# Attention as woven lists of steps with a stated matmul order, a merged softmax and values in two passes

## The chip, the cores and the metric

The kernel runs on one core of a Trainium2 chip. The metric is device time in microseconds (us), the median of several runs. Engines: PE is TensorE (matmuls and transposes), DVE is VectorE, ACT is ScalarE, POOL is GpSimd, and SP is SyncE, which issues most DMAs. Each engine takes its instructions strictly in the order of its own list.

## The reference, cut to what matters

Two layers over 512 latent tokens of width 1024, in f32. Layer 0 is attention: each latent query sees a neighbourhood of the grid (with a learned bias) and 256 context keys in one softmax. Layer 1 is a spatial gating unit; a squared-ReLU MLP follows each. Shifts, scales and gates come from a conditioning vector.

```python
q, k, v = jnp.split(h @ w_qkv, 3, axis=-1)
q = rms_norm(heads(q), q_g)
k = rms_norm(heads(k), k_g)
...
s_lat = jnp.einsum('bjqhd,bkjmhd->bhjqkm', q_r, k_r,
                   preferred_element_type=jnp.float32) * scale + bias[None].astype(jnp.float32)
s_ctx = jnp.einsum('bjqhd,blhd->bhjql', q_r, kc,
                   preferred_element_type=jnp.float32) * scale
s = jnp.concatenate([s_lat.reshape(s_lat.shape[:4] + (n_lat_keys,)), s_ctx], axis=-1)
p = jax.nn.softmax(s, axis=-1).astype(v.dtype)
...
o = (jnp.einsum('bhjqkm,bkjmhd->bjqhd', p_lat, v_r)
     + jnp.einsum('bhjql,blhd->bjqhd', p_ctx, vc))
...
y = y.transpose(1, 0, 2, 3).reshape(bsz, n_tok, D_MODEL) @ w_o
x = x + g1 * y
x = x + g2 * squared_relu_mlp(modulate(rms_norm(x, norm2_g[i]), sh2, sc2), mlp_w1[i], mlp_w2[i])
```

## The kernel before, in words

**Numbers.** Every f32 operand is split in two parts that the fast matmul takes, `hi` (a rounded copy by ACT) and `lo` (the rest, a subtract by DVE). `products` (L183) multiplies such pairs with three matmuls: high by high, high by low, low by high. Weights come in units of 1536 columns by DMA (`raw`), are split into `whi` (ACT, L80) and `wlo` (DVE, L81) four pieces at a time, and lie in three buffers.

**Stages.** A start (to about 71 us) normalises the input and makes the projections of pair 0. Attention follows, then the output projection (`residual("o", ...)`), the MLP of layer 0, the gating unit, the MLP of layer 1.

**Attention** works on 8 pairs of heads. For a pair, `a_tile` multiplies 6 token tiles (4 latent with 384 columns of q, k and v, 2 context with 256 of k and v) by 8 pieces of weights in a bank of tag "mm", and empties the bank: squares, a raw copy, the values as `vh` and `vl`, sums of squares. `a_final` normalises, then `split` transposes three groups through the two banks of tag "t" (L417): context keys, latent keys, queries; ACT and DVE split each, and 16 small DMAs on SP's queue place the parts for the score matmuls. `scores(n)` does one head: for each of 4 query blocks two matmuls give 512 scores (256 latent, 256 context) in a bank of tag "s"; DVE takes the maximum of the context half (L461) and, with the bias added, that of the latent half (L462), ACT two exponentials (L465, L467), DVE adds the sums and inverts (L469, L470), and POOL scales the block in `pbuf`. `values(n)` does one head: for 6 key tiles, `turn` transposes the weights of 2 to 4 query blocks (L496), ACT and DVE split them into `ph` and `pl` (L499, L500), and `products` multiplies them with the values. The stationary operand is the head's 64 columns beside 64 columns of zeros, and both heads of a pair add up in one bank of tag "o".

**Conditioning products.** Beside this, `ada_block` loads 512 KB of conditioning weights into a single buffer `adaraw` by SP's queue and reduces them on DVE (L338); 24 of the 80 are done in attention, each tied behind a tile's sum of squares.

**Order.** The program calls `scores`, `values`, `a_tile` and `a_final` by pairs, and a scheduler decides at build time, by its own account of times, how their instructions stand in each engine's list. The output projection opens its first four blocks together (`first=4`), three in "mm" banks; the scheduler puts their matmuls among the last heads.

## Time and profile before

| | us |
|---|---|
| median of 3 runs | 1554.05 |
| lowest and highest | 1551.54, 1558.43 |
| the profiled execution | 1556.16 |
| its span, first to last instruction | 1554.4 |

The profile is one execution. Its page shows each engine's busy time over the span; windows show the same for a stretch; groups collect the instructions of a line and operation, with busy time, mean and the idle time before them; the timeline has single instructions. A matmul's length in the timeline includes its passage through the array, and the next one starts well before its end, so the distance of two starts tells what one costs. PEld are weight loads. The granted clock of PE is 1.00 of 2.4 GHz all through attention.

### The profile page before, as it was taken

To read this page: it belongs to the slowest core of one execution; us is meant where nothing else is said; L and a number is where in the kernel's file an instruction comes from. 1 tells how busy PE (TensorE), PEld (TensorE's weight loads), DVE (VectorE), ACT (ScalarE), POOL (GpSimd) and SP (SyncE) were. 2 spreads that over 40 slices of the span, in tenths; PEclk is the share of its full clock that TensorE was granted. 3 is DMA by queue.
4 is the path that set the end of the run, shared out by engine and by line. 5 is a ranking of instruction groups with operands and counts; after the bars stand their busy time and mean duration, and the time that the engine had idled before them with its cause. 6 is when DMAs were issued, how large, how long until landed. Compare 5 with 4: busy or idle time off the path is not lost.

```text
span 1554.4 us, 21486 instructions
## 1 busy us (share of the span) xinstructions
PE 1508.7 (97%) x7960; PEld 1290.6 (83%) x7960; DVE 925.4 (60%) x1953; ACT 663.6 (43%) x1569; POOL 135.8 (9%) x162
## 2 busy tenths in 40 slices
PE   3999999999999999999999999999999999999999
PEld 2898888887888888878978887888889988888888
DVE  5778777776776555765565568644456743334431
ACT  3566666675554312442343356323234542234320
POOL 0222222211200000000100013100001000000000
PEclk9999999999999999999999999999999999999999
DMA  9465555544246555555234235323221422223230
GB/s 321 145 177 169 164 167 162 164 115 161 74 143 202 187 199 191 197 196 191 85 125 135 98 100 166 123 90 111 93 95 42 143 102 93 90 102 102 99 112 27
DMA packets 69224, 212.08 MB, mean 136 GB/s; under 512 B 8320, under 2 KB 27392, under 8 KB 68736
## 3 DMA queue, kind: packets, MB, share of 16 engines
q1 hardware_dynamic: 57600, 200.57, 39.5%
q10 hardware_dynamic: 11520, 10.15, 2.1%
q8 instruction: 62, 1.02, 0.3%
q14 instruction: 42, 0.34, 0.1%
HBM read 193.91 MB, written 2.10 MB: 126 GB/s over the span
## 4 chain that ended last, share of the span: by engine, by line
PE 55%; DMA 12%; DVE 5%; issue 2%; ACT 0%; ACTq 0%; DVEq 0%
PE ps_mm L183 27%; PE ps_t L183 18%; DMA adaraw<-ada 11%; PE ps_o L183 9%; DVE adaraw L338 2%; PE ps_s L713 1%; DVE wlo L81 1%; DVE nt L172 0%; DMA raw<-wall 0%; DVE xall L569 0%; PE ps_s L156 0%; DVE acc L151 0%; DVE hl L174 0%; DVE relu L620 0%; DVE mod L338 0%
## 5 line engine op out<-in xcount | busy, mean ns | idle before, releaser
L80 ACT CAST whi<-raw 128x384 fp32r<-128x384 f32 x620 | 278.3, 510 | 358.0 <-PE ps_mm L183 142.1
L81 DVE TENSOR_TENSOR wlo<-raw,whi 128x384 fp32r<-128x384 f32 x620 | 329.5, 579 | 146.0 <-ACT whi L80 145.7
L338 DVE CUSTOM_DVE_ANT_0 adaraw<-adaraw,cb 128x1024 f32<-128x1024 f32 x80 | 99.2, 1240 | 105.0 <-DMA adaraw<-ada 104.9
L183 PE MATMUL ps_mm<-hh,wlo 128*128 128x512 f32 (+1 forms) x416 | 154.0, 370 | 0.6 <-DVE wlo L81 0.6
L183 PE MATMUL ps_mm<-hh,whi 128*128 128x512 f32 (+1 forms) x416 | 154.2, 371 | 0.0
L183 PE MATMUL ps_mm<-hl,whi 128*128 128x512 f32 (+1 forms) x416 | 153.8, 370 | 0.0
L183 PE MATMUL ps_mm<-whi,hh 128*128 128x384 f32 (+1 forms) x344 | 122.4, 358 | 4.0 <-ACT hh L289 4.0
L183 PE MATMUL ps_mm<-mh,whi 128*128 128x512 f32 (+1 forms) x336 | 121.4, 361 | 2.2 <-ACT mh L623 2.2
L183 PE MATMUL ps_mm<-wlo,hh 128*128 128x384 f32 (+1 forms) x344 | 122.1, 355 | 0.1
L183 PE MATMUL ps_mm<-ml,whi 128*128 128x512 f32 (+1 forms) x336 | 121.4, 361 | 0.2 <-DVE ml L624 0.2
L183 PE MATMUL ps_mm<-whi,hl 128*128 128x384 f32 (+1 forms) x344 | 121.5, 356 | 0.0
L183 PE MATMUL ps_mm<-mh,wlo 128*128 128x512 f32 (+1 forms) x336 | 121.1, 360 | 0.0
L183 PE MATMUL ps_t<-hh,whi 128*128 128x512 f32 (+1 forms) x280 | 104.4, 373 | 0.0
L183 PE MATMUL ps_t<-hl,whi 128*128 128x512 f32 (+1 forms) x280 | 104.2, 372 | 0.0
L183 PE MATMUL ps_t<-hh,wlo 128*128 128x512 f32 (+1 forms) x280 | 103.9, 371 | 0.0
L183 PEld LDWEIGHTS ps_mm<-hh,wlo 128*128 128x128 f32 x416 | 78.4, 189 | 13.8 <-DVE wlo L81 0.8
L183 PEld LDWEIGHTS ps_mm<-hl,whi 128*128 128x128 f32 x416 | 78.5, 189 | 12.6
L183 PEld LDWEIGHTS ps_mm<-hh,whi 128*128 128x128 f32 x416 | 78.5, 189 | 12.6
L623 ACT CAST mh<-relu 128x512 fp32r<-128x512 f32 x64 | 39.7, 621 | 99.8 <-DVE relu L620 99.8
L183 PEld LDWEIGHTS ps_mm<-mh,whi 128*128 128x128 f32 x336 | 63.7, 190 | 12.2 <-ACT mh L623 2.7
L183 PEld LDWEIGHTS ps_mm<-whi,hh 128*128 128x128 f32 x344 | 65.2, 190 | 9.0 <-ACT hh L289 4.4
L183 PEld LDWEIGHTS ps_mm<-ml,whi 128*128 128x128 f32 x336 | 63.9, 190 | 10.2 <-DVE ml L624 0.5
(217 smaller groups left out, 3303.6 us busy)
## 6 DMA issues: line engine op xcount, KB each, us to landing
raw<-wall SPq DMA_DIRECT2D x155, 768.0 KB, 4.5
adaraw<-ada SPq DMA_DIRECT2D x80, 512.0 KB, 3.9
aw<-ada SPq DMA_DIRECT2D x32, 256.0 KB, 7.1
bt<-bias_t SPq DMA_DIRECT2D x16, 512.0 KB, 3.5
q<-th SPq DMA_DIRECT2D x32, 128.0 KB, 2.4
q<-tl SPq DMA_DIRECT2D x32, 128.0 KB, 2.4
bc<-lngb ACTq DMA_DIRECT2D x12, 256.0 KB, 3.4
x0l<-x0T SPq DMA_DIRECT2D x2, 1024.0 KB, 9.3
```

The costliest lines, as they stand in the source:

```text
L80: nc.scalar.copy(out=hi[:, cs], in_=raw[:, cs])
L81: nc.vector.tensor_tensor(out=lo[:, cs], in0=raw[:, cs], in1=hi[:, cs], op=ALU.subtract)
L183: pe.matmul(o, lhsT=a, rhs=b, start=start and i == 0, stop=stop and i == n - 1, skip_group_check=shared)
L338: vec.tensor_tensor_reduce(out=a, in0=a, in1=cb, scale=1.0, scalar=0.0, op0=ALU.mult, op1=ALU.add, accum_out=mod[:, idx:idx + 1])
L623: act.copy(out=a, in_=r)
L713: pe.matmul(s[:, n * P:(n + 1) * P], lhsT=v[:, n, g * P:(g + 1) * P], rhs=ws, start=True, stop=True)
```

## The change

- **Values.** `vv` holds, for a token tile, high and low values side by side: for head 0 as (high, low), for head 1 as (low, high). One head's 128 columns are the stationary operand of two matmuls, with `ph` and with `pl`; the sum of the high part stands in one half of the bank's partitions and that of the low part in the other. `finish` copies the low half to `side` (ACT) and adds it to the high half (DVE), once for each head, and so the bank "o" belongs to one head at a time.
- **Softmax.** One DVE pass over all 512 scores gives the negated scores with bias (zero for the context) and their minimum, one exponential over 512 follows with the sum of its outputs; one reciprocal for the four blocks of a head, and then the four scalings on POOL.
- **Order.** Attention becomes lists of steps: `a_steps` (one token tile by one piece of weights), `f_steps` (normalise, then the three transposed groups), `s_steps` (one query block), `v_steps` (one key tile, with the products a step behind the transposes), `o_steps` (one block of the output projection by one pair). `weave` puts a list of fill between the steps of another. Every matmul and transpose in them goes through `InOrder`, so PE's list keeps the program's order; the other engines' lists are the scheduler's as before.
- **Output blocks.** Four blocks are opened during the last two pairs and serve as fill there: three in "mm" banks, one in a bank of "s".
- The context keys are normalised first; `W.ahead` is 1 in the last head.

```diff
+    in_order = tc.keep_in_program_order
+    class InOrder:
...
+        def __getattr__(self, name):
+            f = getattr(self.engine, name)
+            return lambda *a, **k: in_order(f(*a, **k))
...
-    vh = [[at.tile([P, 192], F32R, name=f"vh{b}_{t}") for b in range(NV[t])] for t in range(6)]
-    vl = [[at.tile([P, 192], F32R, name=f"vl{b}_{t}") for b in range(NV[t])] for t in range(6)]
+    vv = [[at.tile([P, 256], F32R, name=f"vv{b}_{t}") for b in range(NV[t])] for t in range(6)]
...
+    pe_ = InOrder(pe)
...
+    def a_steps(p, ts):
...
+        def step(t, k):
+            if k == 0:
+                open_[t] = mm()
+            qkv_products(open_[t], t, W.get("qkv", p * KC + k), k, eng=pe_)
+            if k == KC - 1:
+                evict(p, t, open_[t])
...
+            for i, n in ((2, 4), (0, 8), (1, 8)):
...
-            vec.reduce_max(sm[:, 0, jc], s[:, 256:], axis=AX.X)
-            vec.tensor_tensor_reduce(out=pb[:, 64:320], in0=s[:, :256], in1=bt[:, j], scale=1.0,
-                                     scalar=sm[:, 0, jc], op0=ALU.add, op1=ALU.max, accum_out=sm[:, 1, jc])
...
-            vec.tensor_tensor(out=sm[:, 4, jc], in0=sm[:, 2, jc], in1=sm[:, 3, jc], op=ALU.add)
...
+            vec.tensor_tensor_reduce(out=pb, in0=s.rearrange("p (s k) -> p s k", s=2), in1=bt[:, j:5:4 - j], scale=-1.0,
+                                     scalar=3e38, op0=ALU.add, op1=ALU.min, accum_out=m[:, 0, jc])
+            act.activation(out=pb, in_=pb, func=AF.Exp, scale=-1.0, bias=m[:, 0, jc], accum_out=m[:, 1, jc])
+            if j == 3:
+                vec.reciprocal(out=m[:, 2], in_=m[:, 1])
+                for i in range(4):
+                    pb = pbuf[(4 * n + i) % NPB]
+                    pool.tensor_scalar(out=pb[:, 64:], in0=pb[:, 64:], scalar1=m[:, 2, i:i + 1], scalar2=0.0,
+                                       op0=ALU.mult, op1=ALU.add)
...
-            products(o[:, cs], [((vh[kt][b][:, vs], vl[kt][b][:, vs]), (ph, pl))],
-                     h == 0 and i == 0, h == 1 and i == 5)
...
+            for a, part in enumerate((ph, pl)):
+                pe_.matmul(o[0][:, cs], lhsT=vv[kt][p % NV[kt]][:, vs], rhs=part, start=i == 0 and a == 0,
+                           stop=i == 5 and a == 1)
...
+            act.copy(out=side, in_=o[0][other])
...
+                vec.tensor_tensor(out=rowmajor(OT[p][main]), in0=grid(o[0][main]), in1=grid(side), op=ALU.add)
...
+    def weave(main, fill):
+        for i, e in enumerate(main):
+            e()
+            for f in fill[i * len(fill) // len(main):(i + 1) * len(fill) // len(main)]:
+                f()
...
+        s = s_steps(2 * p)
+        v = v_steps(2 * p - 1) if p else []
+        if p + 1 < NPAIR:
+            fill = a_steps(p + 1, (5, 2, 3))
+        else:
+            fill = o_steps(range(3), range(2, 5))
+        weave(v[:2] + s[:2] + v[2:3] + s[2:] + v[3:], fill)
+        s = s_steps(2 * p + 1)
+        v = v_steps(2 * p)
+        if p + 1 < NPAIR:
+            f = f_steps(p + 1)
+            if p + 2 < NPAIR:
+                fill = a_steps(p + 2, (0, 1, 4))
+            else:
+                for k in range(6):
+                    o_halves(k)
+                fill = o_steps(range(3), range(2))
+            weave(f[:1] + s[:2] + v[:1] + s[2:] + v[1:2] + f[1:2] + v[2:3] + f[2:3] + v[3:4] + f[3:] + v[4:], fill)
+        else:
+            o_halves(6)
+            weave(s[:2] + v[:1] + s[2:] + v[1:], o_steps(range(3), range(5, 7)))
+    W.ahead = 1
+    weave(v_steps(2 * NPAIR - 1), o_steps((3,), range(7)))
+    for f in o_steps(range(4), (7,)):
+        f()
```

PE's list before, in the values of a head in the middle of attention (`pb` are blocks of weights to transpose, `vh` and `vl` the values' parts, the number a tile):

```order
L183 MATMUL ps_o<-ph,vh_5_669 128x512
L183 MATMUL ps_o<-pl,vh_5_669 128x512
L183 MATMUL ps_o<-ph,vl_5_683 128x512
L496 MATMUL ps_t<-ident,pb_712 128x128
L496 MATMUL ps_t<-ident,pb_713 128x128
L496 MATMUL ps_t<-ident,pb_714 128x128
L183 MATMUL ps_o<-ph,vh_0_657 128x256
L183 MATMUL ps_o<-pl,vh_0_657 128x256
L183 MATMUL ps_o<-ph,vl_0_671 128x256
```

PE's list of the change, at the fourth and fifth key tile of a head (`hch` and `hcl` are the context's parts, by weights of the next pair but one):

```order
L186 MATMUL ps_t<-ident,pb_675 128x128
L186 MATMUL ps_t<-ident,pb_676 128x128
L186 MATMUL ps_t<-ident,pb_677 128x128
L186 MATMUL ps_o<-ph,vv_1_661 128x384
L186 MATMUL ps_o<-pl,vv_1_661 128x384
L186 MATMUL ps_mm<-whi,hch_116 128x256
L186 MATMUL ps_mm<-wlo,hch_116 128x256
L186 MATMUL ps_mm<-whi,hcl_124 128x256
L186 MATMUL ps_t<-ident,pb_676 128x128
L186 MATMUL ps_t<-ident,pb_677 128x128
L186 MATMUL ps_o<-ph,vv_2_664 128x384
L186 MATMUL ps_o<-pl,vv_2_664 128x384
```

Of three matmuls for a key tile two are left, and between a tile's transposes and its products stand the products of the tile before and three of the projection.

DVE's list before, behind the fourth score block of a head, in the second half of a pair (`sm` holds maxima and sums, `adaraw` the conditioning weights, `tl` the low part of transposed keys or queries):

```order
L469 TENSOR_TENSOR sm<-sm 128x1
L464 TENSOR_SCALAR sm<-sm 128x1
L81 TENSOR_TENSOR wlo<-raw,whi 128x384
L470 RECIPROCAL sm<-sm 128x1
L389 TENSOR_TENSOR vl_0_670<-ps_mm,vh_0_656 128x2x64
L390 TENSOR_REDUCE ss<-sqa 128x4
L338 ISA adaraw,mod<-adaraw,cb 128x1024
L338 ISA mod 128x1
L421 TENSOR_TENSOR tl<-ps_t,th 128x512
```

DVE's list of the change, from the third score block on in the same half (`pl` is the low part of transposed weights, which PE's second value matmul takes):

```order
L487 ISA pb_680,sm<-ps_s,bt 128x2x256
L487 ISA sm 128x1
L525 TENSOR_TENSOR pl<-ps_t,ph 128x512
L81 TENSOR_TENSOR wlo<-raw,whi 128x384
L391 TENSOR_REDUCE ss<-sqa 128x4
L390 TENSOR_TENSOR vv_0_657<-ps_mm,vv_0_657 128x128
L348 ISA adaraw,mod<-adaraw,cb 128x1024
L348 ISA mod 128x1
L487 ISA pb_681,sm<-ps_s,bt 128x2x256
L487 ISA sm 128x1
L525 TENSOR_TENSOR pl<-ps_t,ph 128x512
L434 TENSOR_TENSOR tl<-ps_t,th 128x256
```

The small steps of the softmax are gone, and the subtracts of the values now stand between score passes, with the conditioning product between two of them.

## Rows read from the trace of the kernel before

**Rows 1.** The page's table of engines: busy us (share of span), instructions.

```profile
PE 1508.7 (97%) x7960; PEld 1290.6 (83%) x7960; DVE 925.4 (60%) x1953; ACT 663.6 (43%) x1569; POOL 135.8 (9%) x162
```

**Rows 2.** Windows: length, each engine's busy us (instructions), PE clock, DMA share, GB/s.

```profile
230.00:270.00 40.00, 39.18 (x245) 35.83 (x245) 31.68 (x100) 25.64 (x77) 9.06 (x10) 1.00 0.55 166
...
350.00:386.00 36.00, 34.12 (x185) 26.12 (x184) 25.41 (x79) 21.02 (x64) 7.35 (x10) 1.00 0.52 173
```

**Rows 3.** Chain of waits: start us, length us, piece; 48 matmuls of 512 columns.

```profile
783.99 10.88 PE ps_t L183 x48
```

**Rows 4.** Timeline of PE: start us, length us, instruction; 256 columns, then 384.

```profile
215.05 0.28 PE L183 MATMUL ps_mm<-whi,hcl 128*128 128x256 f32 x1
215.17 0.28 PE L183 MATMUL ps_mm<-whi,hch 128*128 128x256 f32 x1
...
230.51 0.33 PE L183 MATMUL ps_mm<-whi,hh 128*128 128x384 f32 x1
230.69 0.33 PE L183 MATMUL ps_mm<-wlo,hh 128*128 128x384 f32 x1
```

**Rows 5.** Waits of PE: who waited for whom, us in total, times, longest.

```profile
PE ps_t L417 <- DVE tl L421: 3.5, 5, 0.8
```

**Rows 6.** Groups of PE by form: instruction, count, busy us, mean ns, idle before.

```profile
L183 PE MATMUL ps_o<-ph,vl 128*128 128x512 f32 x32 | 12.7, 396 | 0.0
L183 PE MATMUL ps_o<-ph,vl 128*128 128x384 f32 x32 | 10.8, 339 | 0.0
L183 PE MATMUL ps_o<-ph,vl 128*128 128x256 f32 x32 | 9.0, 282 | 0.0
```

**Rows 7.** Groups of the whole span: a weight load of PE, columns as above.

```profile
L183 PEld LDWEIGHTS ps_mm<-hh,wlo 128*128 128x128 f32 x416 | 78.4, 189 | 13.8 <-DVE wlo L81 0.8
```

**Rows 8.** Timeline of PE at a pair's transposes, around 227 us.

```profile
226.60 0.34 PE L183 MATMUL ps_mm<-wlo,hh 128*128 128x384 f32 x1
227.77 0.63 PE L417 MATMUL ps_t<-ident,raw 128*128 128x128 f32 x4 [0.83 <-DVE tl L421]
```

**Rows 9.** Timelines of PE and DVE at the start of attention.

```profile
71.31 0.34 PE L183 MATMUL ps_mm<-whi,hh 128*128 128x384 f32 x1
...
75.13 2.18 DVE L403 TENSOR_TENSOR raw<-raw,ss 128x512 f32<-128x512 f32 x3
83.93 0.69 DVE L421 TENSOR_TENSOR tl<-ps_t,th 128x512 fp32r<-128x512 f32 x1 [1.32 <-DMA kk<-tl]
...
87.36 0.70 PE L458 MATMUL ps_s<-kk,q 128*128 128x512 f32 x2 [0.44 <-issue]
```

**Rows 10.** Timelines: copy and subtract of one transposed tile; PE near the end.

```profile
196.10 0.48 ACT L499 CAST ph<-ps_t 128x384 fp32r<-128x384 f32 x1 [0.65 <-PE ps_t L496]
...
196.61 0.56 DVE L500 TENSOR_TENSOR pl<-ps_t,ph 128x384 fp32r<-128x384 f32 x1 [0.71 <-ACT ph L499]
...
376.16 0.49 PE L496 MATMUL ps_t<-ident,pb 128*128 128x128 f32 x3
377.45 0.45 PE L183 MATMUL ps_o<-ph,vh 128*128 128x384 f32 x1 [0.81 <-ACT ph L499]
378.14 0.45 PE L183 MATMUL ps_o<-pl,vh 128*128 128x384 f32 x1 [0.24 <-DVE pl L500]
```

**Rows 11.** Groups of DVE from 190 to 270 us, two pairs.

```profile
L338 DVE CUSTOM_DVE_ANT_0 adaraw<-adaraw,cb 128x1024 f32<-128x1024 f32 x8 | 9.8, 1223 | 2.5 <-DMA adaraw<-ada 2.5
L462 DVE CUSTOM_DVE_ANT_0 pb<-ps_s,bt,sm 128x256 f32<-128x256 f32 x17 | 8.0, 478 | 0.1
L461 DVE TENSOR_REDUCE sm<-ps_s 128x1 f32<-128x256 f32 x16 | 6.5, 419 | 0.6 <-PE ps_s L459 0.6
L469 DVE TENSOR_TENSOR sm<-sm 128x1 f32<-128x1 f32 x17 | 4.5, 266 | 1.4 <-ACT pb L467 1.4
```

**Rows 12.** Groups of ACT from 190 to 270 us, two pairs.

```profile
L467 ACT ACTIVATE pb<-pb,sm 128x256 f32<-128x256 f32 x16 | 8.1, 506 | 0.0
```

**Rows 13.** Timeline of DVE: a conditioning product that waited for its load.

```profile
215.54 1.22 DVE L338 CUSTOM_DVE_ANT_0 adaraw<-adaraw,cb 128x1024 f32<-128x1024 f32 x1 [1.53 <-DMA adaraw<-ada]
```

More of the change, by code (lines that the diff above doesn't have):

```diff
@@ L381, in a_tile, with evict @@
+    RAW_BUFS = (2, 1, 2)
+    def evict(p, t, o):
+        st = pairs.setdefault(p, {"raw": {}})
+        if "ss" not in st:
+            st["ss"] = aq.tile([P, 20], F32, tag="ss", bufs=2, name="ss")
         n, s0 = (256, t * 4) if t < 4 else (128, 16 + (t - 4) * 2)
+        i = t // 2
+        if i not in st["raw"]:
+            st["raw"][i] = aq.tile([P, 2, n], F32, tag=f"raw{i}", bufs=RAW_BUFS[i], name=f"raw{i}")
         sq = aq.tile([P, 256], F32, tag="sqa", bufs=2, name="sqa")
         act.activation(out=sq[:, :n], in_=o[:, :n], func=AF.Square)
-        act.copy(out=st["raw"][t // 2][:, t % 2], in_=o[:, :n])
+        act.copy(out=st["raw"][i][:, t % 2], in_=o[:, :n])
@@ L445, in both, with s_steps, step @@
         return kk[:, a:a + 2 * (T - a)].rearrange("p (s k) -> p s k", s=2)[:, :, :256]
-    def scores(n):
+    def s_steps(n):
         p, h = divmod(n, 2)
-        q1, q2, kk = (a[h] for a in pairs[p]["qk"])
-        bt = at.tile([P, 4, 256], F32, tag="bias", bufs=1, name="bt")
-        nc.sync.dma_start(out=bt, in_=bias_t[n])
-        sm = at.tile([P, 5, 4], F32, tag="sm", bufs=2, name="sm")
-        for j in range(4):
-            pb = pbuf[(4 * n + j) % NPB]
+        sm = []
+        def step(j):
+            q1, q2, kk = (a[h] for a in pairs[p]["qk"])
+            if j == 0:
+                nc.sync.dma_start(out=bt[:, :4], in_=bias_t[n])
+                sm.append(at.tile([P, 3, 4], F32, tag="sm", bufs=2, name="sm"))
+            m = sm[0]
+            pb = pbuf[(4 * n + j) % NPB].rearrange("p (s k) -> p s k", s=2)[:, :, 64:]
             s = bank("s", 2)
@@ new lines, in finish, with step @@
+                act.copy(out=rowmajor(oh[p][main]), in_=grid(side))
+                vec.tensor_tensor(out=rowmajor(ol[p][main]), in0=grid(side), in1=rowmajor(oh[p][main]), op=ALU.subtract)
+        def step(i):
+            if i < 6:
+                turn(i)
+            if i > 0:
+                multiply(i - 1)
+            if i == 6:
+                finish()
+        return [lambda i=i: step(i) for i in range(7)]
+    def weave(main, fill):
[3 more added lines that the diff above has]
+                f()
@@ new lines, in o_halves, with o_steps, step @@
+    def o_halves(k):
+        act.copy(out=oh[k], in_=OT[k])
+        vec.tensor_tensor(out=ol[k], in0=OT[k], in1=oh[k], op=ALU.subtract)
+    o_open = {}
+    def o_steps(ms, ks):
+        def step(m, k):
+            if k == 0:
+                o_open[m] = mm() if m < 3 else bank("s", 2)
+            products(o_open[m], [(W.get("o", m * NPAIR + k), (oh[k], ol[k]))], k == 0, k == NPAIR - 1, eng=pe_)
+        return [lambda m=m, k=k: step(m, k) for k in ks for m in ms]
+    for t in range(6):
+        evict(0, t, o0[t])
@@ L561, in normed, with residual @@
         return go
[L563 removed]
+    def residual(sec, K, hi, lo, gate, opened=(), tail=0, nm=None, then=None, dst=None):
         def wts(m):
@@ L598, in residual @@
                     then(c0, c1)
-    for k in range(NPAIR - 1):
-        act.copy(out=oh[k], in_=OT[k])
-        vec.tensor_tensor(out=ol[k], in0=OT[k], in1=oh[k], op=ALU.subtract)
     nm = Norm(xp)
-    residual("o", NPAIR, oh, ol, lambda m: mcol(0, 2, m), first=4, tail=3, nm=nm,
+    residual("o", NPAIR, oh, ol, lambda m: mcol(0, 2, m), o_open, tail=3, nm=nm,
              then=normed(nm, A2[0], lambda k: mcol(0, 3, k)))
```

188 lines of the change are left out of this document (75 added, 113 removed).

## Prediction

> **What bounds the kernel now.** I read the table of engines first: the matrix engine (PE) is busy 97% of the span and the next engine, DVE, 60% [rows 1]. So the question is only what PE still executes and where it waits. The windows say where the attention differs from the rest: in a stretch of 40 us in its middle PE is busy 39.2, DVE 31.7 and ACT 25.6, and in its last 36 us DVE has 25.4 [rows 2]. PE is the bound there too, but DVE stands at 79% with it, so a stated PE order has less slack than the whole-span shares suggest. Busy time of PE hides how pipelined it is; the price of a matmul is the distance from one start to the next. Third, then, start-to-start distances: 48 matmuls of 512 columns in a row take 10.88 us, 226.7 ns each [rows 3]; 384 columns take 175 ns and 256 columns 120 ns [rows 4]. Last, the waits of PE: in the attention they are few, and the largest group is the transposes of the projected keys and queries, 3.5 us in five waits [rows 5]. The chain of waits as a whole is of little use here: it runs through PE and, in the first MLP, through the conditioning loads, which this change leaves as they are.
>
> **The third value pass.** Before, each key tile of a head costs three matmuls: high part of the weights on high values, low on high, high on low. The new layout puts high and low values side by side as 128 columns of one stationary operand, so two matmuls do the same, and an add joins the two halves of the output. What goes is one of the three groups of 32 at each width [rows 6]: 32 x 0.2267 + 32 x 0.175 + 32 x 0.120 = 7.25 + 5.6 + 3.84 = **16.7 us**. All of it lies on PE, nothing hides it, so all of it counts if PE stays the bound.
>
> Weight loads have rows of their own, one of 189 ns for each matmul [rows 7], and the question is whether a dropped matmul gives back its load too. Start-to-start distances of 226.7 and 120 ns leave no place for it between matmuls, so loads are hidden and give nothing [rows 3, 4]; unhidden, the 96 would give 96 x 0.189 = 18 us more. The Trainium skill, page "TensorE: Matmul & The Clock Gate", section "The mechanism", lists that a weight load overlaps with matmuls in flight only where the row groups differ (its text also names a background buffer for weights); all loads here use all rows, so by the list alone they would stand between the matmuls. The trace does not agree: 120 ns for 256 columns has no room for a load.
>
> **The transposes of keys and queries.** Before, all three groups of a pair stand within a few matmuls of each other, and with two banks of the tag "t" the third has to wait for the copies of the first. It reads as one matmul at 226.60 us followed by the next at 227.77, where 0.175 is usual [rows 8]: 1.0 us, once a pair. In the new order six to twelve products stand between the groups. I take out the waits as their sum has it, **3.5 us** [rows 5]; the bound below is nothing, since another wait can take their place.
>
> **The start.** Pair 0's last product ends and pair 1's first starts at 71.31 us [rows 9]. In the new order 18 products of 384 columns stand before the first transposes: 71.3 + 18 x 0.175 = 74.4. What those need is the normalised context keys; DVE begins the three normalising multiplies at 75.13 and needs 2.18 us [rows 9], and the new code takes the context first, an estimated 0.45 us, so 75.6: PE waits 1.2. Then come 18 products (3.1), the keys, and 18 shorter ones (12 x 0.175 + 6 x 0.12 = 2.8), so the queries are transposed at about 82.1, and PE has 18 products of 256 columns (2.1) and stands before the first score at 84.6. In the trace the score starts 3.4 us after DVE begins the low part of the queries (83.93 to 87.36, [rows 9]), the time of eight small DMAs that SP issues in a row; that low part can begin some 1.2 us after the transposes, so the score is ready at 86.8 and PE waits 2.2. Before, PE waits 0.44 us at that score. Net **+3 us**, between +1 and +4.
>
> **Steady pairs.** A transposed tile goes PE, ACT copy, DVE subtract, PE. One that found both engines free took 0.48 us on ACT and 0.56 on DVE, from 196.10 to 197.17 [rows 10]; with the transposes' own 0.27 us that is 1.35 from the last transpose's start to the second pass. The order now fixes how much PE does in between. After the fourth group it is two passes of 384 columns, three products of 256 and two transposes, 0.35 + 0.35 + 0.15 = 0.85; after a new head's first, six products of 256 and four transposes, 1.07, for 512 columns. These two places leave an estimated 0.3 to 0.5 us each in every pair; elsewhere the fill is longer than the chain. I take 0.8 us for each of the six pairs that have projection products to weave in, **+5 us**. The bound below is 0, and above it is 4 us a pair, from the only place in the trace where PE waited for that chain with its helpers busy: transposes at 376.16, first pass at 377.45, second at 378.14 [rows 10], where a covered step takes about 0.9 us in all, so 1.1 too much, at four places a pair.
>
> What shares ACT and DVE with that chain gets lighter. Two DVE passes over 256 columns (478 and 419 ns) become one over 512; from the same operation at 256 and 1024 columns, 478 and 1223 ns [rows 11], I estimate 726. For the eight score blocks of a pair that is 8 x (726 - 478 - 419) = -1.4 us; the adds go (4.5 us in two pairs, -2.25, [rows 11]); the joining add of each head comes, an estimated 0.6 x 2. DVE then has about 29 us of a pair's 36: still 80%. On ACT two exponentials of 256 columns, the latent one 506 ns [rows 12], become one of 512, and one copy of the output becomes two half copies. All of this lies beside PE and I cost it at nothing; if the cover is gone, it is the second rival.
>
> Other additions: the head's bank of the tag "o" must now be emptied after each head, not each pair. Behind it PE has twelve products of 256 columns and eight transposes before the next head writes there, 2.1 us, against a copy and an add of some 1.3: nothing, with 0.7 a pair as the upper bound. The four scalings on POOL now run together after the fourth score; ten steps of PE stand between, so nothing.
>
> **The end.** Pairs 6 and 7 have 28 groups of three output products as fill, where a full pair has 48 groups. In the last 36 us PE had idle time too, 36.00 - 34.12 = 1.9 us, and more inside its modelled busy time [rows 2]. The new order opens one block more before attention ends, and in the second half of pair 6 DVE has the splits of six finished pairs' outputs, two weight units and a pair's normalisation over only some 10 us of PE work. One gives, the other takes: **0**, between -6 (all waits of that stretch gone) and +7 (DVE's time in that half, an estimated 17 us, less PE's).
>
> **The sum.** -16.7 - 3.5 + 3 + 5 + 0 = -12.2 us. The profiled execution took 1556.16 (span 1554.4), so 1544.0 for it; the median of the three runs, 1554.05, lies 2.1 lower, and from it 1541.9. I forecast **1542 us**.
>
> **The rivals.**
> - *The new order fits better than the scheduler's.* No new waits in steady pairs, all of the end's waits gone, the start at +1: -16.7 - 3.5 + 1 - 6 = -25, so 1529. For it: in the window from 230 to 270 us PE is idle for only 0.8 us [rows 2], and ACT and DVE get lighter. Against it: two places in each pair have less fill than the chain needs.
> - *DVE becomes the bound in the second half of a pair.* There the normalisation, two conditioning products, four score passes, six subtracts and three splits share about 18 us of PE, and DVE's part of them is an estimated 16. Then some 1.6 us a pair are lost beyond the 0.8 I allowed, and the end takes its +7 in part: -12.2 + 6 x 1.6 = -2.6, so 1551. For it: DVE at 79% already. Against it: the first half has slack, and DVE's total falls.
> - *Slower: DVE stands still on a conditioning load.* The change states PE's order, while DVE still runs each conditioning product where its list has it, now between two subtracts that PE waits for. That product waits for its DMA, once for 1.53 us [rows 13]; before, the scheduler laid out both lists together. SP issues that load behind the bias load, which waits for the last score pass of the head before. If each of the 24 loads held PE 1 us: -12.2 + 24 = +12, so 1566. It decides from about 0.5 us a load (24 x 0.5 = 12.2 eaten up). For it: one buffer, one SP queue. Against it: eight steps of fill, 5 us, lie between two such products, and the load lands in about 4.
> - *Each dropped weight load counts too*: -12.2 - 18 = -30, so 1524. The rows at 120 ns exclude it but for 0.01. This is what the list in the Trainium skill named above would make of it.
>
> **How the numbers follow.** Chances: the forecast's case 0.50 (1535 to 1547 by its bounds), better fit 0.20, weight loads 0.01, DVE 0.20, slower 0.09. The range for 8 in 10 leaves out about the lower half of the better fit and the slower case: 1527 to 1554. A measurement can tell 0.5%, 7.8 us, from no change, so faster means below 1546.3 and slower above 1561.8. Faster: nearly all of the forecast's case, the better fit and the loads, 0.46 + 0.20 + 0.01 = 0.67. Slower: most of the last rival, 0.07. The rest, 0.26, is the same.
>
> **What would show it.** In the new profile the value matmuls should be 64 at each width, not 96, and their starts 227, 175 and 120 ns apart. PE's waits should name ACT and DVE copies of the transposed weights at the fourth group and at a head's first, each under 0.6 us, and no longer the third transpose of the keys. The first score should start near 87 us. If DVE's share of a 40 us window rises over 85%, the second rival holds; if DVE waits over 1 us for conditioning loads while PE waits for DVE, the third. The forecast is wrong if the distance from attention's start to its end falls by less than 5 or by more than 20 us, or if stages behind it change by over 1 us, since I moved nothing there.

## Result: slower, with the gain spent on new waits

The changed kernel took **1579.34 us** (median of 4), the kernel before on the same chip 1553.74: a ratio of 1.016 with an interval of 1.0147 to 1.0179. Its profiled span is 1577.9 us, 23.5 longer than before. The forecast was 1542 with a range of 1527 to 1554, and slower was to mean above 1561.8.

Starts of instructions in the two timelines say where the 23.5 us lie. Two distances are used from here on. **A** goes from the first score matmul to the first matmul on hidden values of the first MLP: attention with its output stage, so that it doesn't matter how many output blocks are opened early. **B** goes on to the first matmul on gated values (`gh`) of the second layer, and holds the rest of the first MLP.

| us | before | after | change |
|---|---|---|---|
| first score | 87.4 | 88.9 | +1.5 |
| A | 421.5 | 439.3 | +17.8 |
| B | 438.2 | 442.7 | +4.5 |
| all behind | 607.3 | 607.0 | -0.3 |

The table of engines (busy us, share of the span, instructions) answers to [rows 1]:

```profile
PE 1499.7 (95%) x7864; PEld 1284.5 (81%) x7864; DVE 914.3 (58%) x1730; ACT 656.6 (42%) x1451; POOL 132.3 (8%) x135
```

PE has 96 matmuls less and is busy 9 us less, yet the span grew: the change is waiting. DVE's share fell. Two windows of 40 us in the middle of attention, columns as in [rows 2], with PE's clock after the counts:

```profile
190.00:230.00 40.00, 34.62 (x209) 31.69 (x208) 27.22 (x63) 21.54 (x55) 8.59 (x10) 0.96 0.50 152
270.00:310.00 40.00, 35.10 (x210) 32.14 (x209) 27.25 (x64) 22.33 (x56) 6.53 (x8) 0.96 0.50 151
```

Where PE was busy for 39.2 of 40 us it is now busy for 35, and all other engines do less too: nobody is full over 40 us, and everybody waits for somebody. The waits of PE name the two engines (compare [rows 5], whose line is gone):

```profile
PE ps_t L186 <- DVE pl L525: 13.2, 10, 2.5
PE ps_o L186 <- DVE pl L525: 13.1, 16, 1.9
PE ps_o L195 <- ACT mh L692: 4.7, 2, 4.0
...
PE ps_s L186 <- issue: 3.3, 1, 3.3
```

The value matmuls themselves read as forecast, 32 for each of two passes (compare [rows 6]); the waiting stands ahead of the second:

```profile
L186 PE MATMUL ps_o<-ph,vv 128*128 128x512 f32 x32 | 15.6, 487 | 2.8 <-ACT ph L524 2.8
L186 PE MATMUL ps_o<-pl,vv 128*128 128x512 f32 x32 | 14.7, 461 | 10.9 <-DVE pl L525 10.3
```

The low part of the transposed weights (`pl`, DVE's subtract) holds up both the second value pass and, through the two banks of the tag "t", the next transposes: 26.3 us.

Cut at the score groups, a pair is one stretch from its first head's scores to its second's, and one from there to the next pair's:

```profile
173.90:189.50 15.60, 15.18 (x94) 14.38 (x93) 9.50 (x23) 8.68 (x25) 3.87 (x4) 1.00 0.27 94
189.50:217.10 27.60, 23.03 (x140) 21.11 (x139) 20.47 (x45) 15.97 (x39) 5.05 (x6) 0.94 0.59 167
```

DVE (the third pair of numbers) has 9.5 us of work in the first and 20.5 in the second. Of DVE's groups in the second (count, busy us, mean ns, idle before):

```profile
L525 DVE TENSOR_TENSOR pl<-ps_t,ph 128x512 fp32r<-128x512 f32 (+2 forms) x8 | 4.7, 587 | 1.6 <-ACT ph L524 1.6
L81 DVE TENSOR_TENSOR wlo<-raw,whi 128x384 fp32r<-128x384 f32 x6 | 4.2, 723 | 0.0
L348 DVE CUSTOM_DVE_ANT_0 adaraw<-adaraw,cb 128x1024 f32<-128x1024 f32 x3 | 3.6, 1216 | 1.8 <-DMA adaraw<-ada 1.8
...
L391 DVE TENSOR_REDUCE ss<-sqa 128x4 f32<-128x256 f32 (+1 forms) x4 | 1.5, 376 | 0.2 <-ACT sqa L384 0.2
L390 DVE TENSOR_TENSOR vv<-ps_mm,vv 128x128 fp32r<-128x128 f32 x4 | 1.1, 282 | 0.0
```

(Rows at the edges of a window count whole and neighbours overlap, so the groups add up to a little more than 20.5.) One place in the crowded stretch, timelines of DVE and ACT, then of PE:

```profile
193.11 0.27 DVE L416 RECIPROCAL ss<-ss 128x20 f32<-128x20 f32 x1
193.30 0.50 DVE L81 TENSOR_TENSOR wlo<-raw,whi 128x384 fp32r<-128x384 f32 x1
193.72 1.62 DVE L419 TENSOR_TENSOR raw<-raw,ss 128x256 f32<-128x256 f32 x3
195.25 2.12 DVE L81 TENSOR_TENSOR wlo<-raw,whi 128x384 fp32r<-128x384 f32 x2
197.29 0.68 DVE L487 CUSTOM_DVE_ANT_1 pb<-ps_s,bt 128x512 f32<-128x512 f32 x1
197.90 0.08 DVE L487 DVE_READ_ACCUMULATOR2_ANT sm<- 128x1 f32 x1
197.90 0.68 DVE L525 TENSOR_TENSOR pl<-ps_t,ph 128x512 fp32r<-128x512 f32 x1
...
195.62 0.56 ACT L524 CAST ph<-ps_t 128x512 fp32r<-128x512 f32 x1
```

```profile
196.28 0.47 PE L186 MATMUL ps_o<-ph,vv 128*128 128x512 f32 x1
198.63 0.69 PE L186 MATMUL ps_o<-pl,vv 128*128 128x512 f32 x1 [1.88 <-DVE pl L525]
199.12 0.53 PE L186 MATMUL ps_mm<-whi,hh 128*128 128x384 f32 x1
199.44 0.53 PE L186 MATMUL ps_mm<-wlo,hh 128*128 128x384 f32 x1
```

ACT's copy was done at 196.2. DVE came to the subtract at 197.9, since the normalisation, three weight splits and a score pass stood ahead of it. The projection products behind that matmul needed nothing from it. Ten us later the third rival's picture stands in the same pair, DVE and ACT, then PE:

```profile
208.38 1.22 DVE L348 CUSTOM_DVE_ANT_0 adaraw<-adaraw,cb 128x1024 f32<-128x1024 f32 x1 [1.77 <-DMA adaraw<-ada]
...
209.73 0.55 DVE L525 TENSOR_TENSOR pl<-ps_t,ph 128x384 fp32r<-128x384 f32 x1
...
206.45 0.51 ACT L524 CAST ph<-ps_t 128x384 fp32r<-128x384 f32 x1
```

```profile
207.51 0.28 PE L186 MATMUL ps_mm<-whi,hcl 128*128 128x256 f32 x1
210.33 0.55 PE L186 MATMUL ps_t<-ident,pb 128*128 128x128 f32 x3 [2.54 <-DVE pl L525]
```

DVE stands on a load for 1.77 us and then multiplies for 1.22, and PE stands for 2.54. The Trainium skill, page "PSUM — Partial Sum Buffer", section "Engine vs sequencer instructions", says that the queues of ScalarE, VectorE and GpSimd are strictly first in, first out; these rows agree: the subtract's input was there at 207.0, and it began at 209.7.

### The profile page after: what moved, and what is told of

Same layout as the page of the kernel before. It is cut to its first block, busy times and chain, and to the rows that moved or that the text cites. A ratio compares the mean times of both kernels' runs of the same rounds, so it can differ in the third digit from the quotient of the medians.

```text
span 1577.9 us, 20899 instructions
## 1 busy us (share of the span) xinstructions
PE 1499.7 (95%) x7864; PEld 1284.5 (81%) x7864; DVE 914.3 (58%) x1730; ACT 656.6 (42%) x1451; POOL 132.3 (8%) x135
## 4 chain that ended last, share of the span: by engine, by line
PE 64%; DMA 12%; DVE 9%; issue 4%; ACT 4%; POOL 0%; SPq 0%; ACTq 0%; DVEq 0%; POOLq 0%
PE ps_mm L195 28%; PE ps_t L195 17%; DMA adaraw<-ada 11%; PE ps_o L195 8%; PE ps_mm L186 5%; DVE adaraw L348 2%; DVE wlo L81 2%; DVE pl L525 2%; PE ps_o L186 1%; PE ps_s L186 1%; PE ps_s L782 1%; DMA kk<-tl 1%; PE ps_t L186 1%; DVE pb L487 1%; ACT whi L80 1%
## 5 line engine op out<-in xcount | busy, mean ns | idle before, releaser
L195 PE MATMUL ps_mm<-hh,whi 128*128 128x512 f32 (+1 forms) x376 | 140.3, 373 | 0.0
L195 PE MATMUL ps_mm<-hh,wlo 128*128 128x512 f32 (+1 forms) x376 | 139.6, 371 | 0.0
L195 PE MATMUL ps_mm<-hl,whi 128*128 128x512 f32 (+1 forms) x376 | 139.6, 371 | 0.0
L195 PE MATMUL ps_t<-hh,wlo 128*128 128x512 f32 (+1 forms) x312 | 112.9, 362 | 0.6 <-DVE wlo L81 0.6
L195 PE MATMUL ps_t<-hl,whi 128*128 128x512 f32 (+1 forms) x312 | 113.4, 363 | 0.0
L186 PE MATMUL ps_mm<-whi,hh 128*128 128x384 f32 x224 | 78.1, 349 | 0.0
L186 PE MATMUL ps_mm<-whi,hl 128*128 128x384 f32 x224 | 76.4, 341 | 0.0
L186 PE MATMUL ps_mm<-wlo,hh 128*128 128x384 f32 x224 | 76.4, 341 | 0.0
L646 DVE SCALAR_TENSOR_TENSOR xall<-ps_mm,mod,xall 128x512 f32<-128x512 f32 (+1 forms) x46 | 30.5, 667 | 78.2 <-PE ps_mm L195 77.4
L195 PEld LDWEIGHTS ps_mm<-mh,wlo 128*128 128x128 f32 x336 | 64.1, 191 | 9.6
```

The source lines that it names most:

```text
L186: return lambda *a, **k: in_order(f(*a, **k))
L195: eng.matmul(o, lhsT=a, rhs=b, start=start and i == 0, stop=stop and i == n - 1, skip_group_check=shared)
L646: vec.scalar_tensor_tensor(out=x[m][:, c0:c1], in0=o[:, c0:c1], scalar=gate(m), in1=x[m][:, c0:c1], op0=ALU.mult, op1=ALU.add)
```

## Experiments

Theory: the stated order makes PE stand at every late `pl`, and DVE is late because a pair's DVE work is bunched in one stretch. Rivals: the arithmetic edits themselves cost it; DVE stands on conditioning loads; the single chain copy - subtract is too long for the fill. Each median stands beside the ratio to the kernel before on the same chip. The medians of the kernel before ran from 1551.6 to 1553.7 us on the chips used, so differences between rows are good to about 2 us, and the ratios are free of that. A, B and "pair" are read from the one profiled execution of each kernel. "Pair" is a fifth of the way from pair 1's first score to pair 6's.

| kernel | time | ratio, interval | A | B | pair |
|---|---|---|---|---|---|
| before | 1553.74 | | 421.5 | 438.2 | 39.4 |
| after | 1579.34 | 1.0163 (1.0147-1.0179) | 439.3 | 442.7 | 41.9 |
| e1 order free | 1549.29 | 0.9985 (0.9976-0.9995) | 408.9 | 442.1 | 38.9 |
| e4 both edits, old program | 1543.53 | 0.9945 (0.9931-0.9960) | 405.0 | 441.6 | 37.5 |
| e3 softmax alone | 1555.41 | 1.0019 (1.0010-1.0029) | 416.8 | 443.1 | 38.9 |
| e2 two passes alone | 1550.63 | 0.9989 (0.9978-1.0000) | 412.1 | 443.3 | 38.4 |
| e5 no conditioning | 1551.57 | 0.9992 (0.9980-1.0003) | 413.4 | 443.1 | 37.6 |
| e7 conditioning late | 1578.82 | 1.0178 (1.0160-1.0195) | 441.4 | 443.2 | 42.3 |
| e15 loads kept | 1563.38 | 1.0063 (1.0046-1.0080) | 423.7 | 444.1 | 38.6 |
| e9 products in first half | 1571.42 | 1.0115 (1.0100-1.0130) | 433.6 | 441.9 | 40.7 |
| e6 splits on POOL | 1590.01 | 1.0239 (1.0224-1.0254) | 445.5 | 443.3 | 41.7 |
| e8 one step later | 1572.22 | 1.0118 (1.0100-1.0136) | 433.0 | 441.6 | 41.1 |
| e12 transposes early | 1580.75 | 1.0177 (1.0161-1.0192) | 439.1 | 444.0 | 40.6 |
| e13 both moves | 1570.43 | 1.0112 (1.0097-1.0127) | 431.2 | 441.9 | 39.0 |
| e10 shorter load chain | 1548.03 | 0.9954 (0.9937-0.9971) | 407.7 | 443.4 | 37.5 |
| e14 free last tiles | 1536.00 | 0.9895 (0.9878-0.9911) | 404.5 | 433.8 | 37.4 |
| e16 woven, order free, tail | 1543.74 | 0.9945 (0.9930-0.9959) | 409.4 | 433.9 | 39.1 |

**The stated order, undone** (e1), from the changed kernel:

```
-    pe_ = InOrder(pe)
+    pe_ = pe
```

> The changed kernel with one thing undone: the program is still woven step by step, but the order of the matrix engine's instructions in attention is left to the scheduler again. Theory (the stated order turns each low part of the weights that DVE writes late into a stop of the matrix engine, about 33 us of waits and about 6 us at the lower clock behind them): those 39 us come back, 1579 - 39 = 1540, between 1532 and 1548, and the distance between the first scores of neighbouring pairs falls from 42.4 to about 37.5 us. Rival (the arithmetic edits themselves cost it: the joining add, the 512-wide pass, the batched scaling): the order changes little, 1570 to 1585, and the waits on the low parts stay above 4 us a pair.

30 us came back, all of it in A. The theory's 39 was too much, and its range is missed by 1.3 us, since e1 keeps waits of its own (6.9 us on `pl`, instead of 26.3). But the rival is out: the same edits and the same program, only PE's list is the scheduler's again (and with it the other engines' lists, which it lays out beside it). Telling is that DVE stands on conditioning loads longer than in the changed kernel, and PE hardly minds. Waits of DVE in e1's attention (us in all, times, longest), then in the changed kernel's:

```profile
DVE adaraw L348 <- DMA adaraw<-ada: 10.0, 6, 3.0
```

```profile
DVE adaraw L348 <- DMA adaraw<-ada: 4.9, 5, 1.8
```

Nor does the free order spread DVE's work over a pair. In e1 the second stretch still holds 20.6 us of it (176.1 to 200.0 us), but it takes 23.9 us, where the changed kernel's four take 25.5 to 27.6. The kernel before had the work more evenly, 14.3 and 16.8 us in the two stretches of a pair:

```profile
157.50:178.60 21.10, 21.10 (x139) 19.51 (x139) 14.32 (x47) 11.27 (x38) 2.96 (x4) 1.00 0.51 170
178.60:196.90 18.30, 17.48 (x102) 15.41 (x102) 16.83 (x50) 14.38 (x42) 6.10 (x6) 1.00 0.59 157
```

So the bunching comes with the woven program, and the stated order makes PE pay more for it.

**The arithmetic in the old program** (e4 both edits, e3 and e2 one each). Diff of e2's core, against before:

```
-            products(o[:, cs], [((vh[kt][b][:, vs], vl[kt][b][:, vs]), (ph, pl))], ...)
+            for a, part in enumerate((ph, pl)):
+                pe.matmul(o[:, cs], lhsT=vv[kt][p % NV[kt]][:, vs], rhs=part, ...)
```

and of e3's:

```
-            vec.reduce_max(...); vec.tensor_tensor_reduce(...); two act.activation(...)
+            vec.tensor_tensor_reduce(out=pb, in0=s..., in1=bt[:, j:5:4 - j], ..., op1=ALU.min, ...)
+            act.activation(out=pb, in_=pb, func=AF.Exp, scale=-1.0, bias=m[:, 0, jc], ...)
```

> The kernel before with only the two arithmetic edits, the merged softmax and the values in two passes; the program's order and the end of attention stay as they were. Theory (the stated order is the cause): the third value pass comes off whole, 1554 - 16.7 = 1537, between 1530 and 1545. Rival (the arithmetic edits cost it): 1554 or more, with waits of the matrix engine on the low parts of the weights of over 2 us a pair.

> The kernel before with the merged softmax alone (one 512-wide pass of DVE, one exponential, four scalings together after a head's fourth block); values stay in three passes, the program's order as before. Prediction's step (DVE and ACT get lighter beside other work, worth nothing by itself): attention's length stays within 1.5 us of 299.8, the time within 4 us of before, 1550 to 1558. Rival (part of the 16.4 us that both edits took off attention is the softmax's): 5 us or more off.

> The kernel before with the values in two passes alone; softmax and order as before. Prediction's step (96 dropped matmuls count whole, 16.7 us): from the first score to the first MLP matmul with hidden values 421.5 - 16.7 = 404.8 us, between 402 and 408, and a time of 1537 to 1545. Rival (the joining copy and add take part of it, and the softmax gives the rest): 408 to 414 us there, and 1543 to 1550.

e4's 1543.5 us lie in the theory's range. A fell by 16.5 us with both, by 4.7 with the softmax alone and by 9.4 with the passes alone. So the 16.7 is there, but only with both, and the agreement is partly luck: alone, the passes, which bring a joining copy and add to ACT and DVE, give 7 less than forecast, and the softmax, which I had priced at nothing, gives 4.7. (That it does so by making DVE lighter is argued, not shown; PE's wait for the transposes of keys and queries falls from 3.5 us to 1.0 in e3.) By A, e2 lies in the rival's range (408 to 414) and e3 just short of the rival's 5 us; the times, 1550.6 and 1555.4, miss e2's rival by 0.6 and lie in the range of the prediction's step in e3. For a part of the gains does not arrive: B grew by 3.4 to 5.1 us in all three, which is why e3 is no faster than before.

**The conditioning blocks.** e5 drops the 24 loads and products, e15 keeps the loads and cuts the products to 32 columns, e7 puts each product one projection tile behind its load:

```
-                ada_block(4 * (p - 1) + t)
+                ada_block(4 * (p - 1) + t, True)      # e5: neither load nor product
+                ada_block(4 * (p - 1) + t, 32)        # e15: load, product of 32 columns
+                ada_late(4 * (p - 1) + t)             # e7: product of the tile before, then the load
```

> The changed kernel without the 24 conditioning products of attention and their loads; this leaves that work out (the modulation values of those columns are constants). Rival of the conditioning load (DVE stands still on the load while the matrix engine waits for the low parts queued behind it): most of the 26 us of waits on low parts go, 1545 to 1556. Theory (the stated order meets any late DVE pass, whatever stands ahead of it): DVE loses 24 x 1.3 = 31 us of work, a seventh of what it does in a pair, so the waits shrink by a third or less, 1565 to 1573.

> The changed kernel with each conditioning product of attention moved one projection tile later than its load, so that no product waits for its load; all the work is kept. Rival of the conditioning load: as without the products, less 24 x 1.3 us of DVE work that lies beside other work, 1550 to 1562. Theory of the stated order: DVE's waits on those loads (about 3 us in five pairs) were a small part; 1574 to 1580, and the waits on the low parts keep at least 20 of their 26 us.

> The changed kernel with the 24 conditioning loads of attention kept and the product of each cut from 1024 columns to 32 (this leaves 31/32 of that arithmetic out). Theory (DVE's pass of 1.3 us is what stops the matrix engine): as without loads and products, 1548 to 1557. Rival (the loads' traffic, or their place on SP's queue ahead of the bias and key loads): as the changed kernel, 1568 to 1580.

Without the blocks 27.8 us come back, more than the theory allowed and in the rival's range; with the loads kept, 16.0, between the two ranges. Taken in this order, DVE's passes cost 16 us and the loads 12; the other order, products without loads, was not tried. Of the 12, about 7 lie at the first score and in pair 0 (88.7 and 43.8 us, against 86.4 and 39.0 in e5) and 5 in pairs 1 to 5. One form that they take, e15 shows on DVE:

```profile
243.02 0.19 DVE L348 CUSTOM_DVE_ANT_0 adaraw<-adaraw,cb 128x32 f32<-128x32 f32 x1 [2.15 <-DMA adaraw<-ada]
243.13 0.08 DVE L348 DVE_READ_ACCUMULATOR2_ANT mod<- 128x1 f32 x1
243.13 0.88 DVE L525 TENSOR_TENSOR pl<-ps_t,ph 128x384 fp32r<-128x384 f32 x2
```

A pass of 0.19 us keeps a subtract waiting for 2.15: DVE runs ahead now, reaches the product earlier and stands on its load for longer (9.7 us in attention). But making the products late enough never to stand on a load gave nothing at all: in e7 DVE's products waited 0.6 us instead of 4.9 (3.8 more are put down to two subtracts behind such a load), and the time stayed, as the theory had it. So standing on a load is one form of being late among several: taken away alone, it is replaced (PE still waits 24.5 us on `pl` in e7). Whether the loads' traffic, or their place on SP's queue, has a part in the 12 is not shown. What the passes and these waits have in common is DVE's time in the crowded stretch. The two stretches of a pair in e5:

```profile
163.00:177.90 14.90, 14.90 (x93) 14.36 (x92) 8.26 (x21) 8.66 (x24) 2.93 (x4) 1.00 0.11 37
177.90:200.50 22.60, 21.55 (x140) 19.63 (x140) 16.39 (x39) 15.81 (x39) 4.73 (x6) 1.00 0.63 175
```

With 16.4 us of DVE instead of 20.5 the second stretch takes 22.6 us, not 25.5 to 27.6. (The expectations speak of 20.3 us of matrix work there; here PE is busy for 21.6.)

**The same work elsewhere** (e9):

```
-        if p > 0 and t < 4 and 4 * (p - 1) + t < 24:
+        if p > 0 and (t in (5, 2, 3) or t == 4 and p in (2, 4, 6)):
```

> The changed kernel with the same 24 conditioning products and loads, but 21 of them at the projection tiles of a pair's first stretch, where DVE is busy for 9.3 us of 16, and 3 at a tile of the second, instead of 12 and 12. Theory (uneven share): 9 products of 1.3 us leave the crowded stretches, 1579 - 9 x 1.1 = 1569, between 1563 and 1573. Rival (any DVE pass of 1.3 us ahead of a low part stops the matrix engine, wherever it stands): 1577 to 1581.

7.9 us for nine products moved, with all work and all loads kept: 0.9 us each, as the theory had it, but partly by luck. In pairs 1 to 5, where the theory speaks, it is 1.2 us a pair for 1.5 products, 0.8 each. Another 3.6 us come at the first score (85.3 us; 1.7 of them were won before attention began), and about as much is lost again in pair 6 and around 967 us, where the granted clock is 0.5.

**Relief and order inside the crowded stretch.** e6 gives the weight splits to POOL, e8 puts the value passes one step later, e12 puts a head's first transposes ahead of the normalisation, e13 is e12 with e9:

```
-                nc.vector.tensor_tensor(out=lo[:, cs], ...)
+                (nc.gpsimd if self.on_pool else nc.vector).tensor_tensor(out=lo[:, cs], ...)   # e6
-            if i < 6: turn(i)
-            if i > 0: multiply(i - 1)
+            if i > 1: multiply(i - 2)
+            if i < 6: turn(i)                                                                  # e8
-            weave(f[:1] + s[:2] + v[:1] + s[2:] + v[1:2] + ...
+            weave(v[:1] + f[:1] + s[:2] + s[2:] + v[1:2] + ...                                 # e12
```

> The changed kernel with the low parts of the weight units in attention (6 to 8 subtracts of 128x384 a pair, 0.68 us each) taken by POOL instead of DVE. Theory (with the order stated, DVE's work of a pair falls as 20.4 us beside 20.3 us of matrix work into the stretch from a pair's second score group to the next pair's first, and 9.3 us into the other): DVE loses some 4 us of each such stretch, and the stretches shrink from 26.5 us towards 22 to 24: 1579 - 6 x 3 = 1561, between 1553 and 1567. Rival (DVE has time enough, only the length of the single chain copy - subtract against the next step counts): at most 6 us come back, 1573 or more.

> The changed kernel with the two value passes of each key tile one step later in the stated order, so that a step of projection products more lies between the transposes and the matmuls that use their low parts. Rival (length of the single chain copy - subtract): the waits of the value matmuls on low parts (13 us) vanish and the transposes' waits stay, 1560 to 1567. Theory (DVE's work falls unevenly on the two stretches of a pair): DVE is as late as before, the waits turn up at the transposes and the scores, 1572 to 1580.

> The changed kernel with one step of the stated order moved: in the second half of a pair the first transposes of the head whose values are multiplied stand ahead of the normalisation and of the score blocks, not behind two of them. Theory (at this place the low part of the weights stands on DVE behind a normalisation, weight splits and score passes, about 5 us in a row, and the value matmul stops for 1.9 to 2.4 us, with a stretch at half clock behind it): that stop goes, six times 2 us and some of the half clock, 1579 - 12 - 4 = 1563, between 1558 and 1570. Rival (DVE is late by its load, wherever the step stands): the stop turns up at the next step that needs DVE, 1574 to 1581.

> The changed kernel with both moves: the first transposes early, and the conditioning products in a pair's first stretch. Theory (two causes that add): 1579 - 8 - 14 = 1557, between 1550 and 1563, no value matmul waiting over 1 us at a head's first step. Rival (both moves relieve the same stop): no better than the better of the two alone, 1563 to 1571.

e6 failed the other way, 11 us slower and outside both ranges. Its rows, POOL's splits in one crowded stretch, and DVE's conditioning products in five pairs:

```profile
L81 POOL TENSOR_TENSOR wlo<-raw,whi 128x384 fp32r<-128x384 f32 x6 | 7.9, 1348 | 0.0
```

```profile
L348 DVE CUSTOM_DVE_ANT_0 adaraw<-adaraw,cb 128x1024 f32<-128x1024 f32 x18 | 26.8, 1487 | 3.6 <-DMA adaraw<-ada 3.5
```

A split takes POOL 1.35 us, where DVE took 0.72; DVE's products went from 1314 ns to 1487 beside it. DVE still lost some 2 us of work in the stretch, and the stretch did not shrink. POOL also holds the scalings of the weights and the gains of keys and queries, and PE's transposes now wait 8.0 us for the subtracts of keys and queries; whether that is the whole loss was not tried. It lies at the ends: a pair in the middle takes 41.7 us, against 41.9 in the changed kernel, but the first score comes 2.4 us later, and pairs 0 and 6 take 4.2 and 3.1 us more. The Trainium skill, page "GPSIMD Engine Reference", section "4.1 Engine selection", has POOL about twice as slow on two inputs; 1.35 against 0.72 agrees.

e8 came 7 us faster, at the edge of the theory's range (1572 to 1580), so the length of the single chain counts for something. Its waits moved as the theory said. The waits on `pl` of the value matmuls, 13.1 us, are off its list, and the transposes' grew from 13.2 to 21.7:

```profile
PE ps_t L186 <- DVE pl L525: 21.7, 17, 3.3
PE ps_s L186 <- DVE sm L487: 4.4, 7, 1.3
```

In e12 the first stop goes (no wait instead of 1.9 us) and another one stands a few steps behind, 1.9 to 2.0 us at the transposes; the steady pair wins 1.3 us, but pair 0, where PE waits for POOL's scalings of the weights, loses 5.7 us where the five win 6.7. e13 takes the steady pair to 39.0 us and the time no further than e9 alone. So the times follow the rivals, but the pairs do not: in pairs 1 to 5 the two moves add (1.3 us in e12, 1.2 in e9, 2.9 in e13), as the theory had it. What they win there is lost at the ends: pair 0 takes 45.7 us in e13 (43.1 in the changed kernel), and pair 6 41.7 (37.7), where PE waits 5.5 us for DVE's score passes. The order of the steps does count; a kernel with the ends mended was not tried.

**The first MLP** (e10, e14 from e4; e16 from e1):

```
-    mlp(0, "a", 24, 80, ...)
+    mlp(0, "a", 28, 80, ...)                                      # e10, four blocks at pair 7's tiles
-                    for _ in range(2):
+                    for _ in range(2 if half == 0 else int(m < 11)):   # e14, e16
...
+                while fin and nxt < ada_to:
+                    with tc.issue_after(last.ins):
+                        ada_block(nxt)
+                    nxt += 1
```

> The kernel before with the two arithmetic edits (1543.5) and four of the first MLP's 56 conditioning loads and products moved to the projection tiles of pair 7. In the first MLP these loads run through one buffer, one after another, 5.4 us each, and its last hidden tiles wait 4.4 us for the last of them. Theory (that chain is why the first MLP got 3.5 us longer once attention got shorter): the chain loses 4 x 5.4 us, the wait goes, 1537 to 1541. Rival (the wait is the copy's or the clock's own, not the chain's): it stays, 1542 to 1547.

> The kernel before with the two arithmetic edits (1543.5), in which the conditioning products that stood on DVE's list ahead of the last four hidden tiles of the first MLP's second half stand behind them; the same work, loads and order elsewhere. Theory (each of these tiles' squared activations waits on DVE behind a product that waits for its load, 4.9 us of matrix waits at the end of the hidden tiles, with 6.8 us at half clock behind): the wait falls under 1 us and the half clock goes, 1543.5 - 4 - 3.4 = 1536, between 1533 and 1540. Rival (the wait is the last tile's own chain of copies): the wait stays above 3 us, 1541 to 1546.

> The changed kernel with the matrix engine's order left to the scheduler (1549.3) and the last four hidden tiles of the first MLP freed of the conditioning products ahead of them, as in the old program (1536.0). Theory (the rest between the two programs lies in attention alone): 1549 - 7.5 = 1541.5, between 1539 and 1544. Rival (with the tail freed both programs end together): 1535 to 1538.

The end of the hidden tiles in the changed kernel, DVE and PE:

```profile
715.55 1.23 DVE L348 CUSTOM_DVE_ANT_0 adaraw<-adaraw,cb 128x1024 f32<-128x1024 f32 x1 [0.38 <-DMA adaraw<-ada]
716.70 0.08 DVE L348 DVE_READ_ACCUMULATOR2_ANT mod<- 128x1 f32 x1
716.70 0.69 DVE L689 SCALAR_TENSOR_TENSOR relu<-ps_t,relu 128x512 f32<-128x512 f32 x1
```

```profile
713.69 0.39 PE L195 MATMUL ps_o<-mh,wlo 128*128 128x512 f32 x1
718.09 0.80 PE L195 MATMUL ps_o<-mh,whi 128*128 128x512 f32 x1 [4.01 <-ACT mh L692]
```

The last tile's activation stands on DVE behind a product that waits for its load. Taking four blocks off the chain (e10) brought nothing (ratio 0.9954, where e4 has 0.9945): one product still stood ahead of each of the last tiles, and the wait stayed at 4.2 us. Putting the products behind the last four tiles (e14) took B from 441.6 to 433.8, below that of before. That is the version that beats both kernels: **1536.0 us**. The woven program with a free order and the same tail (e16) ends at 1543.7, in its theory's range; its remaining 7.7 us are in A (4.9) and in the first score and the rest.

## Why the prediction was wrong

By the sum the first matmul on hidden values, at 508.9 us before, would have come 12.2 earlier, at 496.7, and nothing would have changed behind. It came at 528.2, 31.5 us late, and B grew by 4.5.

- **Third value pass, -16.7.** The groups read as forecast, 64 matmuls at each width, and in e4 the 16.5 us are there. The size was right for the two edits together, which is partly luck; alone the passes give 9.4 and the softmax 4.7.
- **Transposes of keys and queries, -3.5.** Their wait is gone from the list, but its bound was the truth: another wait on the same two banks took its place, 13.2 us.
- **Start, +3.** Near: the waits are 1.1 and 3.3 us (forecast 1.2 and 2.2), less the 0.44 of before +4.0, at the upper bound, and the first score stands at 88.9 (forecast 86.8). The third rival has a part here too: DVE begins the low part of the queries at 85.77, behind a conditioning product that waited 1.12 us for its load, and in e5, without these products, at 83.42 (0.7 of the difference is an earlier start).
- **Steady pairs, +5: the step that failed.** Two mistakes. First, I followed one tile's chain against the fill behind it, with ACT and DVE free. In the rows above the subtract itself takes 0.68 us, and the queue ahead of it several. Second, when the second rival did count DVE, I listed "the normalisation, two conditioning products, four score passes, six subtracts and three splits", 16 us. In the crowded stretch (which reaches a little into the next half) the trace has 20.5: the list left out the weight splits (4.2 us), the projections' own passes (1.5 + 1.1) and the joining add. In pairs 1 to 5 the trace gives 41.9 us a pair, against 37.5 for the same arithmetic in the old program: 4.4 lost instead of 0.8, beyond the 4 that I had named as the upper bound. (Six pairs at that bound make 1561 by my own sum; my range left that out.) Pair 0 comes on top, and I had priced it like the others: 43.1 us from its first score to the next pair's, 31.9 in e4. By the matmul counts and the distances above, 4 to 5 us of this are an estimate of the work that the old order does ahead of the first score; the rest is waits, 0.8 on a query's DMA, 1.3 on POOL's scalings and 3.8 on `pl`, and a stretch at half clock.
- **The end, 0.** From pair 6's first score to the first matmul on hidden values the changed kernel takes 186.6 us, the kernel before 192.9: 6 us less, of which the value passes of two pairs are some 4. That is within the bounds.
- **Rivals.** Two of them describe the rows: DVE bound in the second half (1551) and DVE on a conditioning load (1566). (The first one's text lets the end take part of its +7, its sum does not.) I priced them as alternatives; they add, because both are the same thing, DVE late while PE can't go around. The third rival's price of 1 us a load was near: 28 us for 24 blocks, passes included. Its chance, 0.09, was not.
- **DVE over 85% of a 40 us window** was the wrong sign to look for: the two windows above show 68%. A stretch in which two engines wait for each other shows neither full.
- **Behind attention, 0.** I moved nothing there and B still grew 4.5 us. In the kernel before, the same wait was there, at 2.2 us:

```profile
PE ps_mm L183 <- ACT mh L623: 2.2, 1, 2.2
```

It grew in every kernel whose tail was not freed, also in those whose edits touch attention alone. The 56 conditioning products there take 299 to 301 us from first to last in the four kernels read for it (after, e1, e4, e5), 293 in the kernel before, with the same start relative to the MLP. Why the chain runs 2% slower is open.

## What to carry to other kernels

A stated order on the busiest engine can take from it what covered the lateness of the others (here 30 us of it): before stating it, add up the work of each feeding engine between two steps of that order, all of it, loads waited for included, and not only the chain of the item at hand. Shared work that isn't urgent (splits of later weights, products behind a load) belongs where the feeding engine has slack, or behind the last step that is waited for. And a gain in one stage should be followed to the end of the next: here a single wait at the first MLP's end swallowed a fifth (e4) to all (e3) of it until its cause was moved.

## What was not expected of the hardware

Behind some stops PE's granted clock falls. In the kernel before the granted clock is 0.5 (1.2 GHz) in no stretch of attention; in the changed kernel it is in four, 3.4 us each, from 89.6, 198.8, 284.1 and 366.0 us: 13.7 us at half speed, so about 6.8 us lost that no wait shows. The first follows the 3.3 us before the first score, the second the 1.88 us shown above, where 384 columns then start 0.32 us apart instead of 0.175. At the first MLP's end 6.8 us at half clock follow the 4.0 us stop. In e8 it is 27.3 us in attention. Stops of like length were not all followed by a fall: in e9 one of 1.88 us that ended at 151.8 was not, nor was the one of 2.54 us shown above, and what tells them apart was not tried.
